# Two layers of a four-branch decoder trunk: the last recurrence unit's serial steps as block diagonal products of the whole array

## The chip, the cores and the metric

The kernel runs on one core of a Trainium2 chip. The core has five engines that run on their own and meet through semaphores: TensorE multiplies matrices (PE in the profile, and PEld for its loading of weights), VectorE (DVE), ScalarE (ACT) and GpSimd (POOL) do elementwise work, SyncE (SP) issues DMAs. The metric is the device time of one execution in microseconds (us), and the median of several executions is what counts.

TensorE holds one operand of a product, the weights, and streams the other one through. In the profile a form such as `128*128 128x512` says how large the array is that the product uses (rows * columns) and how large the streamed operand is. `64*64` is one quarter of the array.

## The reference

Two layers, each with four parallel branches that read the same 512 tokens of 1024 channels. The change lies in one branch, the RWKV-7 time mixing, whose core is a recurrence over tokens, for 8 heads of width 64:

```python
def step(state, inp):
    r_t, w_t, k_t, v_t, a_t, b_t = inp
    sa = jnp.einsum('bhvk,bhk->bhv', state, a_t)
    state = (state * w_t[:, :, None, :] + sa[..., None] * b_t[:, :, None, :]
             + v_t[..., None] * k_t[:, :, None, :])
    return state, jnp.einsum('bhvk,bhk->bhv', state, r_t)
...
_, y = lax.scan(step, s0, xs)
y_mu = jnp.mean(y, -1, keepdims=True)
y_var = jnp.mean(jnp.square(y - y_mu), -1, keepdims=True)
y = ((y - y_mu) * lax.rsqrt(y_var + RWKV_GN_EPS)).reshape(B, S, W) * lnx_g + lnx_b
```

The other branches are latent attention, a convolution module and cross-attention into a memory. Each branch's output is gated, projected to 1024 channels, weighted by a sigmoid of the layer's input and added up; one more projection, the residual and a layer norm end the layer.

## The kernel before

**Tiles and streams.** All large products run on TensorE with operands split into a high and a low part, three products for one (`mm3`): tiles `ps_m` (merge gates), `po` (branch projections), `ps_rg` (gates of the recurrence branch), `pz` (last projection). These make up one long stream of items, written out at the end of `layer_items`. Each product of that stream has the form 128*128 with a streamed operand of 128x512.

**The recurrence in units.** The scan is turned into chunks of 64 tokens. `rwkv_unit(j0, hf, rkv)` (L764) treats two pairs of heads (`SUB`, index `s`) over 256 tokens, that is 4 chunks; `un = j0 + hf` numbers the four units of a layer 0 to 3, and units 1 and 3 go on with the state that units 0 and 2 left. The two heads of a pair lie on partitions 0 to 63 and 64 to 127 (`HALF`). Within a unit the order is: small products of 64x64 that solve within each chunk (tiles `g`, `x0`, `x1`, `x2`, `va`), then `gb`, from which VectorE makes for every chunk the transition `Gs` (identity added), the input `H` and the readout `B` (L1062 to L1069); then the serial steps (L1073 to L1089): in each, `w = Gs^T state` on TensorE, then `S = w * decay + H` on VectorE. Step c+1 reads the S of step c. Unit 3 has three such steps, c = 0, 1, 2. Then the readout `yb` (L1093), the statistics over each head (`bn_stats`, `bn_aggr`, L1109 to L1115), a power on GpSimd, the normalisation on ScalarE, and transposes `ty` back (L1125). All products inside a unit are quarter-array products (`64*64`); in a step, four of them: two pairs of heads by two heads.

**What sets the order.** The program is written out by a planner in Python: `Plan` keeps a clock for each engine from a table of costs, and the order in which it emits instructions is the program order on each engine. The stream of large products is the filler; units and other side work are tasks, each of which says what it waits for when it yields. A task that yields "pe" is taken up as soon as its time has come on TensorE's clock; one that yields "small" moreover waits until `GATHER` = 1500 ns have passed since the array was last used in quarters (L161), so that quarter-array work of several tasks goes out in one group. One that yields "slack" waits until VectorE's planned clock is reached (L157): other work on VectorE goes first. `plan.due` sets a task's time to that at which given tiles are ready. `shape` (L110) charges the switch of the array between quarters and whole. `MM` (L271) chooses the cost of a product by its form; the one for a full-precision product of the whole array is 1.667 ns for each streamed column and 5 ns more (L284).

**Counters.** `L["chains"]`, `L["backs"]`, `L["ends"]`, `L["units"]` count, within a layer, the units that have gone through the readout, the solve, the transposes, and everything. Tiles in the recurrence's pool carry tags, and one tag with `bufs=1` is one buffer: `Q`, `M` and `T` are such tags, and `yb` takes `T` (L1099).

**The stream around unit 3.** In layer 0 unit 3 comes while the third branch's merge items (`ps_m`, `po`) run, in layer 1 while the recurrence branch's gate items (`ps_rg`) run. The gated outputs of the recurrence branch are needed by the last merge items, `merge_items(0, ...)`, which stand behind the four `ps_rg` items and two `ps_m` items.

Of the kernel before, what the change touches and what calls it, by code (L numbers as in the profile page):

```python
# [16 lines left out]
ALU = mybir.AluOpType  # L17
# [181 lines left out]
def _names(*aps):  # L199
    return [a.tensor.name for a in aps if hasattr(a, "tensor")]  # L200
# [65 lines left out]
def trunk_kernel(ctx: ExitStack, tc: tile.TileContext, A, out, dbg=None):  # L266
    nc = tc.nc
    plan = Plan(tc.keep_in_program_order)
    V, S, G = Engine(plan, nc.vector, "DVE"), Engine(plan, nc.scalar, "ACT"), Engine(plan, nc.gpsimd, "POOL")

    def MM(o, lhsT, rhs, start, stop, four=False):  # L271
        n = 1
        for d in rhs.shape[1:]:
            n *= d
        k, m = lhsT.shape[0], lhsT.shape[-1]
        plan.shape(64 if k <= 64 else 128, 64 if m <= 64 else 128)
        if max(k, m) <= 64:
            c = max(0.42 * n + 1.0, 29.0) if four else max(0.83 * n + 12.0, 59.0)
        elif rhs.dtype != F32 or n < 16:
            c = max(0.4167 * n + 13.0, 109.0) * (2 if rhs.dtype == F32 else 1)  # L280
        elif m <= 64:
            c = 0.83 * n + 3.0
        else:
            c = 1.667 * n + 5.0  # L284
        plan.op("PE", c, _names(o), _names(lhsT, rhs))
        plan.keep(nc.tensor.matmul(o, lhsT, rhs, start=start, stop=stop))  # L286
# [13 lines left out]
    def pool(bufs, **k):  # L300
        return Space(plan, ctx.enter_context(tc.tile_pool(bufs=bufs, **k)), bufs)
# [8 lines left out]
    pa = pool(2, name="pa", space=PSUM)  # L310
# [28 lines left out]
    def cc(n):  # L339
        return cst[:, CCOL[n][0]:CCOL[n][1]]  # L340
# [227 lines left out]
    HALF = [slice(0, 64), slice(64, 128)]  # L568
# [70 lines left out]
    def layer_items(l):  # L639
        items = []  # L640
        L = {}
# [109 lines left out]
        SUB = range(2)  # L751

        def chunks(ap):

            return ap.rearrange("p (a b) w -> p b a w", b=2)

        def by2(ap):
            return ap.rearrange("p (a b) w -> p a b w", a=2)
# [5 lines left out]
        def rwkv_unit(j0, hf, rkv):  # L764
            t = f"_{l}_{j0}_{hf}"
            un = j0 + hf
# [6 lines left out]
            def rk(tag, shape, name=None, dt=F32, bufs=1):  # L773
                return L["rp"].tile([128] + shape, dt, tag=tag, name=(name or tag) + t, bufs=bufs)
# [27 lines left out]
            bt, kt, w = rk("bt", [2, 256]), rk("kt", [2, 256]), rk("s4", [2, 256], "w")  # L802
# [16 lines left out]
            for s in SUB:  # L819
                for cp, c2, h in quads:  # L820
                    c = 2 * cp + c2
                    MM(g0[HALF[c2], h, 128 * s + 64 * cp:128 * s + 64 * cp + 64], bt[HALF[h], s, 64 * c:64 * c + 64], AR[HALF[h], s, c, 0], start=True, stop=True, four=True)
            for s in SUB:
                for cp, c2, h in quads:
                    c = 2 * cp + c2
                    MM(g0[HALF[c2], h, 256 + 2 * s + cp:257 + 2 * s + cp], sq[HALF[h], s, 64 * c:64 * c + 64], bones2[HALF[h], h:h + 1], start=True, stop=True, four=True)
            gvs = [g1[:, :, 256 * s:256 * s + 256].rearrange("p h (a w) -> p h a w", a=2) for s in SUB]
            for s in SUB:
                for cp, c2, h in quads:
                    c = 2 * cp + c2  # L830
# [7 lines left out]
            M = rk("M", [8, 65]).rearrange("p c w -> p (c w)")[:, 0:512].rearrange("p (s c w) -> p s c w", s=2, c=4)  # L838
            gm = g0[:, :, 0:256].rearrange("p h (s c w) -> p s h c w", s=2, c=2)
            for cp in range(2):  # L840
                V.tensor_tensor(out=M.rearrange("p s (a b) w -> p s a b w", b=2)[:, :, :, cp], in0=gm[:, :, ::-1, 1] if cp else gm[:, :, :, 0],
                                in1=rn[:, :, cp:4:2].unsqueeze(3).to_broadcast([128, 2, 2, 64]), op=ALU.mult)
# [55 lines left out]
            for s in SUB:  # L898
                yield "slack"
                V.tensor_tensor(out=NQ[s].rearrange("p (h a) m w -> p h a (m w)", h=2), in0=gvs[s],  # L900
                                in1=mask.unsqueeze(1).unsqueeze(1).to_broadcast([128, 2, 2, 128]), op=ALU.mult)
# [38 lines left out]
            def place(tag, name):  # L940
# [12 lines left out]
            T, Q, Zd = (rk(n, [2, 4, 64]) for n in "TQZ")  # L953
            V.tensor_tensor(out=T.rearrange("p s c (b t) -> p (s c) b t", b=4), in0=tc_.unsqueeze(2).to_broadcast([128, 8, 4, 16]),
                            in1=bm.unsqueeze(1).unsqueeze(3).to_broadcast([128, 8, 4, 16]), op=ALU.mult)
# [13 lines left out]
            for s in SUB:  # L969
                for cp, c2, h in quads:  # L970
                    c = 2 * cp + c2
# [47 lines left out]
                    MM(x2[HALF[h ^ cp], 1, s, c2, h], NQ[s][HALF[c2], 2 * h + cp, 0], vt[s][HALF[c2], 2 * h + cp], start=True, stop=True, four=True)  # L1019
            L["backs"] += 1  # L1020
            yield
            Z = rk("Z", [2, 4, 64], "Zi")
            for c2, copy in ((0, S.copy), (1, V.tensor_copy)):
                copy(Z.rearrange("p s (a b) w -> p b s a w", b=2)[:, c2], x2[:, 0, :, c2])
                for s in SUB:
# [6 lines left out]
            for s in SUB:  # L1032
                for cp, c2, h in quads:
                    MM(va[HALF[c2], s, h ^ cp, cp], Z[HALF[h ^ cp], s, 2 * cp + c2], RA[s][HALF[h ^ cp], 2 * c2 + h], start=True, stop=True, four=True)
            yield
# [7 lines left out]
            gb, hh, y0 = ([x[:, :, a:b].rearrange("p c (a w) -> p c a w", a=2) for x in gbs] for a, b in ((0, 256), (256, 384), (384, 512)))  # L1043
            for s in SUB:
                for cp, c2, h in quads:
                    MM(gb[s][HALF[h], c2, cp], VA[s][HALF[c2], 2 * (h ^ cp) + cp, 64:128], BP[s][HALF[c2], 2 * h + cp], start=True, stop=True, four=True)
                for cp in range(2):
                    for first in (True, False):
                        for c2 in range(2):
                            for h in range(2):  # L1050
                                e = 2 * h + cp
                                x, y = (bk1[s][:, e], vt[s][:, e]) if first else (BP[s][:, e, 0:64], VA[s][:, 2 * (h ^ cp) + cp, 0:64])
                                MM(hh[s][HALF[h], c2, cp], x[HALF[c2]], y[HALF[c2]], start=first, stop=not first, four=True)
                for h in range(2):
                    for first in (True, False):
                        for cp in range(2):
                            for c2 in range(2):
                                e = 2 * h + cp
                                x, y = (NQ[s][:, e, 1], vt[s][:, e]) if first else (BP[s][:, e, 64:128], VA[s][:, 2 * (h ^ cp) + cp, 0:64])
                                MM(y0[s][HALF[c2 ^ cp], c2, h], x[HALF[c2]], y[HALF[c2]], start=first, stop=not first, four=True)  # L1060
            yield
            Gs, H, B, Y0 = (rk(tag, [2, 4, 64], n) for tag, n in ((n, n) for n in ("Gs", "H", "B", "Y0")))  # L1062
            for s in SUB:
                V.tensor_tensor(out=by2(H[:, s]), in0=hh[s], in1=chunks(dl[:, 4 * s:4 * s + 4]).to_broadcast([128, 2, 2, 64]), op=ALU.mult)
                V.tensor_tensor(out=by2(Gs[:, s]), in0=gb[s][:, :, :, 0:64], in1=cc("id2")[:, 0:64].unsqueeze(1).unsqueeze(1).to_broadcast([128, 2, 2, 64]), op=ALU.add)
                S.copy(by2(Y0[:, s]), y0[s])
            for s in SUB:
                V.tensor_tensor(out=by2(B[:, s]), in0=gb[s][:, :, :, 64:128], in1=chunks(AR[:, s, :, 1, :]), op=ALU.add)
# [4 lines left out]
            states = [[zero, zero] if hf == 0 else [state[j] for s, j in js]]  # L1073
            for c in range(4):
                e = 2 * (c % 2) + c // 2
                if hf == 0 and c == 0:
                    states.append([H[:, s, 0] for s in SUB])
                elif hf == 0 or c < 3:
                    ps, = yield from pa.take([128, 2, 64], f"w{c}" + t, 1, "small")
                    for s in SUB:  # L1080
                        for half in HALF:
                            MM(ps[half, s], Gs[half, s, e], states[c][s][half], start=True, stop=True)
                    yield
                    s1 = rk("S", [2, 64], f"S{c}", bufs=4)
                    for s in SUB:
                        V.scalar_tensor_tensor(out=s1[:, s], in0=ps[:, s], scalar=dl[:, 4 * s + c], in1=H[:, s, e], op0=ALU.mult, op1=ALU.add)
                    pa.free()
                    states.append([s1[:, s] for s in SUB])
                    yield  # L1089
            for s, j in js:  # L1090
                state[j] = states[-1][s]
            yield lambda: un == 3 or L["backs"] > un + 1
            ps, = yield from pg.take([128, 2, 512], "yb" + t, 1, "small")  # L1093
            yp = ps[:, :, 0:256].rearrange("p h (s a w) -> p s h a w", s=2, a=2)
            for s in SUB:
# [11 lines left out]
            bs, mv = rk("gs", [48]), rk("gm", [16])  # L1107
            y8 = yb.rearrange("p s e w -> p (s e) w")
            for e in range(8):  # L1109
                if e % 2 == 0 and un < 3:  # L1110
                    yield "slack"
                V.bn_stats(bs[:, 6 * e:6 * e + 6], y8[:, e])
            if un < 3:
                yield "slack"
            for e in range(8):  # L1115
                V.bn_aggr(mv[:, 2 * e:2 * e + 2], bs[:, 6 * e:6 * e + 6])
# [8 lines left out]
            ps, = yield from pa.take([128, 512], "ty" + t)  # L1125
# [29 lines left out]
        def rkv_items(j):  # L1155
            def take(n, i):
                def after(ps):
                    d = u(f"{n}{j}" + t_)
                    mix(4 * i + j, ps, d)
                    rkv[j][n] = d  # L1160
                    if n == "v" and j % 2:
                        for hf in range(2):
                            plan.spawn(rwkv_unit(j - 1, hf, rkv[j - 1:j + 1]))
                return after

            for i, n in enumerate("rkv"):
                ch_item(4 * i + j, f"{n}{j}", take(n, i), lambda: "lora" in L and (j < 2 or L["read"] or room()))
# [940 lines left out]
```

## Time and profile before

| | |
|---|---|
| median of 3 runs | 1488.05 us (1487.92 to 1488.8) |
| the profiled execution, its own time | 1488.66 us |
| its span, first to last instruction | 1486.5 us |
| mean granted TensorE clock | 0.998 |
| recurrence steps of unit 3, layer 0 (starts) | 583.66, 586.31, 590.10 us |
| recurrence steps of unit 3, layer 1 (starts) | 1346.79, 1349.43, 1352.08 us |

The busy times of the profile's first part are those of all instructions of an engine, as shares of the span. Rows of a timeline give the start, the duration and the count of instructions that stand next to each other; the duration of a product runs from its start to its modelled end, and products overlap, so that the distance from one start to the next is what a product costs on a full TensorE. A bracket at the end of a row is the time that the engine sat idle before it, and what released it. A full-precision product appears as two records: the four products of a step are a row with x8.

### The profile page before, as it was taken

The numbers are of one execution on the slowest core, as the hardware profiler recorded it, in microseconds if no ns is written. First come the engines' busy times: TensorE is split into PE (matmuls) and PEld (weight loads), VectorE is DVE, ScalarE is ACT, GpSimd is POOL, SyncE is SP. The second block draws the span as 40 slices with busy tenths as digits, with TensorE's granted clock in tenths as the row PEclk, the third lists the DMA queues.
The fourth block names the chain that finished last, engine by engine and source line by source line (L and its number), as shares of the span: only waits on it lengthen the run. The fifth ranks groups of instructions, "written<-read, shape, count | busy, mean of one in ns | idle before, by whom it ended". The sixth has DMA issues, their size and how long they took to land.

```text
span 1486.5 us, 29014 instructions
## 1 busy us (share of the span) xinstructions
PE 1472.0 (99%) x11818; PEld 1232.9 (83%) x11818; DVE 1043.4 (70%) x1994; ACT 675.6 (45%) x1303; POOL 144.2 (10%) x329
## 2 busy tenths in 40 slices
PE   9999999999999999999999999999999999999997
PEld 8888888888888887888999888888888788888886
DVE  5799998755757666545554899997866476757747
ACT  5546653425354534343264465623454354444331
POOL 0000000020403030000010000000040203121002
PEclk9999999999999999999999999999999999999999
DMA  6444342332232222433353252332232313233532
GB/s 215 137 125 101 86 125 85 99 75 89 73 91 73 84 82 89 127 118 129 112 164 109 75 147 65 115 102 97 89 95 76 95 49 107 68 103 118 163 96 78
DMA packets 89158, 153.50 MB, mean 103 GB/s; under 512 B 41025, under 2 KB 47425, under 8 KB 89025
## 3 DMA queue, kind: packets, MB, share of 16 engines
q1 hardware_dynamic: 89024, 151.65, 34.3%
q8 instruction: 93, 1.52, 0.4%
q14 instruction: 41, 0.33, 0.1%
HBM read 134.32 MB, written 5.77 MB: 94 GB/s over the span
## 4 chain that ended last, share of the span: by engine, by line
PE 91%; DVE 4%; ACT 1%; DMA 1%; POOL 1%; issue 1%; SPq 0%; DVEq 0%; ACTq 0%; POOLq 0%
PE ps_m L286 24%; PE po L286 12%; PE ps_cg L286 3%; PE ps_xg L286 3%; PE ps_rg L286 3%; PE ps_xq L286 3%; PE ps_mg L286 3%; PE ps_glu L286 3%; PE ps_v L286 3%; PE ps_val L286 3%; PE ps_r L286 2%; PE pz L286 2%; PE ps_k L286 2%; PE ms L286 2%; PE pl L286 2%; PE x L286 1%
## 5 line engine op out<-in xcount | busy, mean ns | idle before, releaser
L235 DVE SCALAR_TENSOR_TENSOR cacc<-hpad,prm,cacc 128x512 f32<-128x512 f32 x240 | 178.9, 748 | 4.0
L235 ACT ACTIVATE tm<-ps_m,prm 128x512 f32<-128x512 f32 x64 | 44.1, 689 | 160.1 <-PE ps_m L286 159.9
L235 DVE SCALAR_TENSOR_TENSOR mt<-tm,po 128x512 f32<-128x512 f32 x48 | 32.9, 686 | 89.8 <-PE po L286 89.7
L235 POOL TENSOR_TENSOR tmpW<-ZT,W 64x14 f32<-64x14 f32 (+6 forms) x112 | 44.2, 395 | 8.0
L235 ACT ACTIVATE mP<-ms,nmm 128x128 f32<-128x128 f32 (+3 forms) x64 | 33.8, 529 | 22.2 <-DVE nmm L235 17.2
L235 POOL TENSOR_SCALAR ZT<-W 64x256 f32<-64x256 f32 x8 | 6.3, 783 | 359.4 <-DMA W<-scr 317.4
L235 POOL TENSOR_TENSOR ZT<-ZT,tmpW 64x14 f32<-64x14 f32 (+6 forms) x112 | 38.9, 348 | 8.8
L235 DVE TENSOR_TENSOR merged<-merged,mt 128x512 f32<-128x512 f32 x48 | 33.2, 692 | 1.7
L235 ACT COPY mPT<-mt 128x128 f32<-128x128 f32 (+3 forms) x64 | 26.8, 427 | 15.2 <-PE mt L291 14.1
L235 POOL MEMSET D<- 128x8 f32 x8 | 0.9, 117 | 332.7 <-PE ms L286 316.7
L235 DVE TENSOR_REDUCE nmm<-ms 128x1 f32<-128x128 f32 (+3 forms) x64 | 30.7, 484 | 0.1
L235 DVE SCALAR_TENSOR_TENSOR merged<-tm,po 128x512 f32<-128x512 f32 x16 | 11.0, 685 | 26.6 <-PE po L286 26.6
L235 POOL TENSOR_SCALAR lrs<-lmv 128x1 f32<-128x1 f32 x8 | 4.0, 501 | 252.6 <-DVE lmv L235 247.6
L291 PE MATMUL mt<-cst,mP 128*128 128x128 f32 x160 | 27.7, 275 | 0.3
L235 DVE TENSOR_SCALAR mP<-mP,smm 128x128 f32<-128x128 f32 (+3 forms) x64 | 24.8, 387 | 2.3
L235 POOL TENSOR_SCALAR gr<-gm 128x8 f32<-128x8 f32 x8 | 2.8, 353 | 223.9 <-DVE gm L235 223.9
L235 ACT ACTIVATE yb<-yb,mr,gr 128x64 f32<-128x64 f32 x64 | 22.1, 430 | 2.4 <-DVE mr L235 2.4
L291 PEld LDWEIGHTS mt<-cst,mP 128*128 128x128 f32 x160 | 18.9, 141 | 4.9 <-issue 1.4
L286 PE MATMUL ms<-kTl,qT 96*128 96x128 f32 (+3 forms) x64 | 22.0, 344 | 0.0
L235 ACT ACTIVATE z<-z,lnb,lrs 128x256 f32<-128x256 f32 (+2 forms) x11 | 7.0, 666 | 30.3 <-DVE lnb L235 30.3
L235 ACT ACTIVATE xP<-xs,nmx 128x256 f32<-128x256 f32 x32 | 15.2, 476 | 12.1 <-DVE nmx L235 11.6
L286 PE MATMUL ms<-kTh,qT 96*128 96x128 f32 (+3 forms) x64 | 20.6, 322 | 0.0
(3575 smaller groups left out, 5251.8 us busy)
## 6 DMA issues: line engine op xcount, KB each, us to landing
w<-in_w_ch_dram SPq DMA_DIRECT2D x146, 512.0 KB, 3.6
w<-in_w_o_dram SPq DMA_DIRECT2D x32, 512.0 KB, 3.6
w<-in_w_out_dram SPq DMA_DIRECT2D x16, 512.0 KB, 3.5
w<-in_w_lat_dram SPq DMA_DIRECT2D x15, 336.0 KB, 3.0
w<-in_w_mk_dram SPq DMA_DIRECT2D x8, 512.0 KB, 3.5
w<-in_w_mv_dram SPq DMA_DIRECT2D x8, 512.0 KB, 3.7
w<-in_w_qk_dram SPq DMA_DIRECT2D x8, 320.0 KB, 3.0
x<-in_xT_dram SPq DMA_DIRECT2D x8, 256.0 KB, 6.2
```

The source lines that it names most:

```text
L235: return self.plan.keep(f(*a, **k))
L286: plan.keep(nc.tensor.matmul(o, lhsT, rhs, start=start, stop=stop))
L291: plan.keep(nc.tensor.transpose(o, i, ident))
```

## The change

Only unit 3 of each layer is treated differently. Two tiles `Gd0` and `Gd1` of 128 partitions by 4 chunks by 128 columns, one for each pair of heads, take the place of `Gs`: the transition of the first head stands in the upper left 64x64, that of the second in the lower right, and GpSimd writes zeros in the other two quarters. They use the buffers of tags `Q` and `M`. A serial step is then one product of the whole array for each pair of heads (weights 128x128, streamed operand 128x64) instead of two of a quarter. Filling takes four additions on VectorE in place of two. The steps are emitted under "pe", after a wait in the planner for the matrix and the state, and no longer under "small". The readout of unit 3 waits in the planner until three units have passed their transposes. The statistics of unit 2 are no longer under "slack".

```diff
             L["backs"] += 1
             yield
+            diag = [rk("Q", [2, 4, 64], "Gd0").rearrange("p s c w -> p (s c w)"), rk("M", [8, 65], "Gd1").rearrange("p c w -> p (c w)")[:, 0:512]] if un == 3 else None
+            if diag:
+                diag = [x.rearrange("p (c w) -> p c w", c=4) for x in diag]
+                for x in diag:
+                    for i in range(2):
+                        G.memset(x[HALF[i], :, 64 - 64 * i:128 - 64 * i], 0.0)
             Z = rk("Z", [2, 4, 64], "Zi")
...
-            Gs, H, B, Y0 = (rk(tag, [2, 4, 64], n) for tag, n in ((n, n) for n in ("Gs", "H", "B", "Y0")))
+            Gs = None if diag else rk("Gs", [2, 4, 64])
+            H, B, Y0 = (rk(n, [2, 4, 64]) for n in ("H", "B", "Y0"))
...
-                V.tensor_tensor(out=by2(Gs[:, s]), in0=gb[s][:, :, :, 0:64], in1=cc("id2")[:, 0:64].unsqueeze(1).unsqueeze(1).to_broadcast([128, 2, 2, 64]), op=ALU.add)
+                eye = cc("id2")[:, 0:64].unsqueeze(1).unsqueeze(1).to_broadcast([128, 2, 2, 64])
+                for i in range(2) if diag else ():
+                    V.tensor_tensor(out=by2(diag[s][HALF[i], :, 64 * i:64 * i + 64]), in0=gb[s][HALF[i], :, :, 0:64], in1=eye[HALF[i]], op=ALU.add)
+                if not diag:
+                    V.tensor_tensor(out=by2(Gs[:, s]), in0=gb[s][:, :, :, 0:64], in1=eye, op=ALU.add)
...
-                    ps, = yield from pa.take([128, 2, 64], f"w{c}" + t, 1, "small")
+                    ps, = yield from pa.take([128, 2, 64], f"w{c}" + t, 1, "pe" if diag else "small")
+                    if diag:
+                        plan.due(*(x for s in SUB for x in (diag[s], states[c][s])))
+                        yield "pe"
                     for s in SUB:
-                        for half in HALF:
+                        if diag:
+                            MM(ps[:, s], diag[s][:, e], states[c][s], start=True, stop=True)
+                        for half in () if diag else HALF:
                             MM(ps[half, s], Gs[half, s, e], states[c][s][half], start=True, stop=True)
...
-            yield lambda: un == 3 or L["backs"] > un + 1
+            yield lambda: L["ends"] >= un if un == 3 else L["backs"] > un + 1
...
-                if e % 2 == 0 and un < 3:
+                if e % 2 == 0 and un < 2:
                     yield "slack"
                 V.bn_stats(bs[:, 6 * e:6 * e + 6], y8[:, e])
-            if un < 3:
+            if un < 2:
                 yield "slack"
```

## The prediction

> **What bounds the kernel now.** I read the page's totals and its chain first, then the span in stretches, then the timeline around the steps of unit 3.
>
> ```profile
> span 1486.5 us, 29014 instructions
> PE 1472.0 (99%) x11818; PEld 1232.9 (83%) x11818; DVE 1043.4 (70%) x1994; ACT 675.6 (45%) x1303; POOL 144.2 (10%) x329
> PE 91%; DVE 4%; ACT 1%; DMA 1%; POOL 1%; issue 1%; SPq 0%; DVEq 0%; ACTq 0%; POOLq 0%
> ```
> ```profile
> core 0: us, PE busy (x) PEld busy (x) DVE busy (x) ACT busy (x) POOL busy (x), PEclk, DMA share, GB/s
> 400.00:600.00 200.00, 199.09 (x2506) 163.30 (x2505) 126.55 (x296) 91.41 (x185) 38.52 (x88) 1.00 0.29 81
> 600.00:1400.00 800.00, 798.58 (x6233) 670.52 (x6232) 547.64 (x1017) 362.45 (x688) 69.68 (x155) 1.00 0.35 106
> 1400.00:1470.00 70.00, 70.00 (x311) 57.96 (x310) 45.32 (x83) 19.82 (x27) 3.25 (x6) 1.00 0.29 91
> ```
>
> TensorE is busy for 1472.0 of 1486.5 us and makes up 91% of the chain that ended last. From 600 to 1400 us it is idle for 800 - 798.58 = 1.42 us, and not at all from 1400 to 1470. So whatever waits for a recurrence step waits behind other products, and a shorter chain of steps by itself earns nothing. The change is worth what it takes from, or adds to, the time that TensorE spends on the steps, plus any new wait of TensorE.
>
> ```profile
> 583.12 0.39 PE L286 MATMUL ps_m<-xh,w90h 128*128 128x512 f32 x1
> 583.35 0.39 PE L286 MATMUL ps_m<-xh,w90l 128*128 128x512 f32 x1
> 583.66 0.45 PE L286 MATMUL w<-S,Gs 64*64 64x64 f32 x8
> 584.04 0.50 PE L286 MATMUL ps_m<-xl,w90h 128*128 128x512 f32 x1
> 584.38 0.39 PE L286 MATMUL ps_m<-xh,w90h 128*128 128x512 f32 x1
> ...
> 586.31 0.45 PE L286 MATMUL w<-S,Gs 64*64 64x64 f32 x8
> 586.69 0.50 PE L286 MATMUL po<-ycg2l,w91h 128*128 128x512 f32 x1
> ...
> 588.19 0.60 PE L291 MATMUL ty<-cst,yb 128*128 128x128 f32 x4
> ...
> 590.10 0.45 PE L286 MATMUL w<-S,Gs 64*64 64x64 f32 x8
> 590.48 0.50 PE L286 MATMUL po<-ycg2l,w91h 128*128 128x512 f32 x1
> ...
> 592.75 0.69 PE L286 MATMUL yb<-S,B 64*64 64x64 f32 x32
> ```
> ```profile
> 1346.47 0.39 PE L286 MATMUL ps_rg<-xh,w214l 128*128 128x512 f32 x1
> 1346.79 0.45 PE L286 MATMUL w<-S,Gs 64*64 64x64 f32 x8
> 1347.17 0.50 PE L286 MATMUL ps_rg<-xl,w214h 128*128 128x512 f32 x1
> 1347.51 0.39 PE L286 MATMUL ps_rg<-xh,w214h 128*128 128x512 f32 x1
> ...
> 1349.43 0.45 PE L286 MATMUL w<-S,Gs 64*64 64x64 f32 x8
> ...
> 1352.08 0.45 PE L286 MATMUL w<-S,Gs 64*64 64x64 f32 x8
> ```
>
> These are the six steps of unit 3, three in each layer. Each stands alone between two products of the large stream: no other quarter-array work shares its group. A large product follows the one before it after 0.23 us (583.12 to 583.35). With a step in between, the way from 583.35 to 584.38 takes 1.03 us for two large products; 1.03 - 2 x 0.23 = 0.57 us is what a lone step costs TensorE, 0.38 us of it from the start of the step to the next large product, the rest the turn of the array into quarters and back. Layer 1 gives the same: 1346.47 to 1347.51 is 1.04 us. **Six steps cost 6 x 0.57 = 3.4 us**, the most that the change can take from the products themselves.
>
> **The new step.** It has two products of the whole array in full precision with 64 streamed columns. No row shows that form, so it is bounded. An x8 row for four products shows two records for one product; I count four records for a new step.
>
> ```profile
> 117.17 0.28 PE L286 MATMUL ms<-kTh,qT 96*128 96x128 f32 x1
> 117.28 0.27 PE L286 MATMUL ms<-kTh,qTl 96*128 96x128 f32 x1
> ...
> 135.69 2.40 PE L286 MATMUL mo<-mPT,v 128*64 128x128 f32 x40
> 138.02 0.33 PE L291 MATMUL mt<-cst,mP 128*128 128x128 f32 x1
> ```
>
> The lower bound comes from the other full-precision product over all 128 rows, `mo`: 40 records from 135.69 to 138.02, 2.33 / 40 = 0.058 us each, so 4 x 0.058 = 0.23 us for a step. That row has weights of only 64 columns, though. With weights of 128 columns the `ms` products, 128 streamed columns in one pass, follow each other after 0.11 us, though a large product streams four times as many columns in 0.23 us, twice the time; there the loading of the weights sets the pace. By that row a new step costs 4 x 0.11 = 0.44 us. If each product of this form needed four records in place of two, it would be 0.87 us. **I take 0.44**: the new weights have 128 columns as those of `ms` have, and 64 streamed columns cannot cover a load which 128 do not. No turn of the array is left to pay, since the neighbours use the whole array too. A step falls from 0.57 to 0.44, 0.13 us; **six give -0.8 us**. The bounds give 6 x (0.23 - 0.57) = -2.0 us and 6 x (0.87 - 0.57) = +1.8 us.
>
> [...]
>
> **VectorE.** Filling the matrices takes four additions where two stood.
>
> ```profile
> 580.04 0.41 DVE L235 TENSOR_TENSOR Gs<-gb,cst 128x256 f32<-128x256 f32 x1
> 580.37 0.41 DVE L235 TENSOR_TENSOR H<-gb_1x,dl 128x256 f32<-128x256 f32 x1
> ...
> 584.16 0.48 DVE L235 SCALAR_TENSOR_TENSOR S<-w,dl,H 128x64 f32<-128x64 f32 x2 [2.06 <-PE w L286]
> ...
> 595.83 1.10 DVE L235 BATCH_NORM_STATS2 gs<-yb 128x6 f32<-128x64 f32 x8
> 596.85 0.62 DVE L235 BATCH_NORM_AGGREGATE gm<-gs 128x2 f32<-128x6 f32 x8
> ```
> ```profile
> L235 DVE SCALAR_TENSOR_TENSOR mt<-tm,po 128x512 f32<-128x512 f32 x48 | 32.9, 686 | 89.8 <-PE po L286 89.7
> ```
>
> One takes 0.33 us from its start to the next (580.04 to 580.37), and the half-height ones stream the same 256 elements, so two more are 0.66 us a layer, 1.3 in all. VectorE has 2.06 us of idle time right behind, and TensorE runs large products meanwhile: cost nothing. Without that cover it would be the 1.3 us. The statistics of unit 2 that now go first are 1.10 + 0.62 = 1.7 us of VectorE work; queued behind them are a merge's addition from `po` and the low part of a weight that is loaded ahead. Who would wait is the large output after next, since these take turns in two banks: the one in between lasts 24 x 0.23 = 5.5 us for a `ps_m` item and 12 x 0.23 = 2.8 us for a `po`, and the emptying of `po`, 0.69 us, behind 1.7 us of statistics needs 2.4: nothing. Were something else ahead of it as well, a `po` would start late, by at most the 1.7 us.
>
> **GpSimd.** Four memsets of 64x256 a layer.
>
> ```profile
> 579.89 0.20 POOL L235 TENSOR_SCALAR gr<-gm 128x8 f32<-128x8 f32 x1 [30.40 <-DVE gm L235]
> 1346.81 0.20 POOL L235 TENSOR_SCALAR gr<-gm 128x8 f32<-128x8 f32 x1 [34.79 <-DVE gm L235]
> ...
> L235 POOL TENSOR_SCALAR ZT<-W x8: 400/788/1212, 312.5 to 1298.1; 64x256 f32<-64x256 f32 x8
> ```
>
> The nearest row, a scaling of 64x256, takes 0.79 us, so 3.2 us; from below, nothing. GpSimd is idle for 30.40 and 34.79 us before its next work in the two layers, and the matrices' additions come only at 580.04: hidden. Without cover, up to 3.2 us of unit 3, still behind large products.
>
> **The waits.** Steps no longer wait for `GATHER`. The readout of unit 3 waits in the planner for the transposes of unit 2, which stood at 588.19, ahead of the readout at 592.75, and come sooner now; nothing on an engine waits, the stream goes on. No DMA is moved, and SP's queue keeps its order. The unit ends some us earlier, which by the idle time above is worth nothing.
>
> **Sum.** 1488.66 (the profiled execution's own time) - 0.8 = 1487.9; that execution lies 0.6 above the median of 1488.05, so the forecast for a median is **1487.2 us**. What a measurement can tell from no change is 0.2%, 3.0 us, thus 1485.1 to 1491.0.
>
> **The rivals.** (a) Cheap products: the step costs 0.23, -2.0 us, 1486.0. For it: the rate of `mo`, and the kernel's own cost table. Against: its weights are half as wide. (b) Dear products: four records each, +1.8, 1489.9. Against: every full-precision row here has two. (c) The other side of the line: TensorE waits. Its queue is in order, and a step placed "pe" has less large work between itself and the S that it needs.
>
> ```profile
> PE tk L291 <- DVE S L235: 1.2, 1, 1.2
> PE w L286 <- DVE S L235: 0.8, 1, 0.8
> ```
>
> The second row shows this wait once, 0.8 us. It decides as soon as fewer than four large products (4 x 0.23 = 0.9) stand between a step and the next, because S takes 0.12 us to start behind the step and 0.48 for the pair (584.04, 584.16). Six gaps of 0.8 (two between steps and one before the readout, in each layer) less 0.8 are +4.0: 1492.1. Behind each waiting step stand all large products of the stream. Against: the step is placed only when the planner reckons S done and adds its latency. (d) A luckier order downstream: from 400 to 1400 us TensorE is idle 0.91 + 1.42 = 2.3 us; if the new order closed all of it as well, -3.1 in all, 1485.0, just beyond the line. Against: the stream is the same list, and only these tasks move. That the change does not do what it says (the steps still alone with turns of the array) would leave 1488.0 and falls into the forecast.
>
> **How the numbers follow.** Forecast 0.46, (a) 0.20, (b) 0.12, (c) 0.12, (d) 0.10. Faster is (d), 0.10; slower is (c), 0.12; the rest, 0.78, lies within 0.2%. The range runs from (d) at 1485.0 to just above (b) at 1490.2, and leaves out (c) and what of (d) falls below.
>
> **What would show it.** Right: the six steps as 128*128 rows of x4, a large product following a step's start after 0.44 us and no gaps of 0.31 or 0.34 around; VectorE with 0.66 us more before the first S; TensorE's idle time in 600 to 1400 near 1.4 us. The page's busy time of TensorE falls by less than 2 us. Wrong: rows of idle time before `w` on PE with S as releaser, records of x8 for the new steps, a step at 0.23, or a late `po`.

## The result and the profile after

The changed kernel takes 1491.19 us in the median of 18 executions (1489.34 to 1492.5), the kernel before 1488.24 us in 18 executions beside them (1487.83 to 1489.2). The ratio is 1.0017, with a 95% interval of 1.0011 to 1.0023: some 2.9 us slower, about the 0.2% that this kernel's measurement can tell, and every execution is longer than the longest of before. The profiled execution took 1492.5 us, 3.8 more than that of before.

The page of the changed kernel, its totals, its instruction queues and its chain (the last by engine):

```profile
span 1490.6 us, 28980 instructions
PE 1473.1 (99%) x11794; PEld 1235.6 (83%) x11794; DVE 1045.7 (70%) x1998; ACT 676.2 (45%) x1303; POOL 146.5 (10%) x337
...
q8 instruction: 93, 1.52, 0.4%
q14 instruction: 40, 0.33, 0.1%
...
PE 85%; DVE 5%; DMA 3%; ACT 3%; POOL 2%; issue 1%; SPq 0%; DVEq 0%; ACTq 0%; POOLq 0%
```

TensorE has 24 products fewer and yet is busy for 1.1 us longer, and its share of the chain fell from 91% to 85%. DMA, VectorE, ScalarE and GpSimd have the difference: something off TensorE ended last for a while. The span in the same stretches as before (columns as there) says where:

```profile
600.00:1400.00 800.00, 795.69 (x6201) 669.13 (x6201) 542.42 (x1003) 360.97 (x685) 69.78 (x160) 1.00 0.36 105
1400.00:1470.00 70.00, 70.00 (x311) 57.97 (x310) 47.82 (x90) 21.50 (x29) 1.57 (x3) 1.00 0.27 86
```

Between 600 and 1400 us TensorE is idle for 800 - 795.69 = 4.31 us, where it was 1.42. The timeline of TensorE around the steps of unit 3, first in layer 0 and then in layer 1:

```profile
585.50 0.40 PE L286 MATMUL po<-ycg1h,w91l 128*128 128x512 f32 x1
585.73 0.56 PE L286 MATMUL w<-S,Gd 128*128 128x64 f32 x4
586.09 0.47 PE L286 MATMUL po<-ycg2l,w91h 128*128 128x512 f32 x1
586.41 0.39 PE L286 MATMUL po<-ycg2h,w91h 128*128 128x512 f32 x1
...
1354.52 0.56 PE L286 MATMUL w<-S,Gd 128*128 128x64 f32 x4
...
1356.36 0.55 PE L286 MATMUL w<-S,Gd 128*128 128x64 f32 x4
```

The way over two large products and a step, 585.50 to 586.41, is 0.91 us; less 2 x 0.23 a step costs 0.45 us, where an old one cost 0.57. (The next large product follows the step's start after 0.36 us and takes 0.32 itself in place of 0.23; the forecast had the cost right and put it all into the first of these.) No step of unit 3 has idle time ahead of it. So the steps did what they were made for, and the loss is elsewhere. The waits of TensorE name it (total, times, longest):

```profile
PE w L286 <- DVE S L235: 2.3, 1, 2.3
PE warm L286 <- POOL reset L235: 1.3, 1, 1.3
PE tk L291 <- DVE S L235: 1.2, 1, 1.2
```

One wait of 2.3 us for a state S is new; the other two are as long in the kernel before. It isn't in unit 3. It stands at 1258 us, in unit 1 of layer 1, whose steps are quarter products as before. The timeline of TensorE there, of before:

```profile
1258.16 0.39 PE L286 MATMUL ps_m<-xh,w202l 128*128 128x512 f32 x1
1258.49 0.52 PE L286 MATMUL w<-S,Gs 64*64 64x64 f32 x8
1258.80 0.69 PE L286 MATMUL x<-Z,P 64*64 64x64 f32 x32
1259.32 0.64 PE L286 MATMUL x<-P,PT 64*64 64x64 f32 x32
```

and of the changed kernel:

```profile
1258.12 0.39 PE L286 MATMUL ps_m<-xh,w202l 128*128 128x512 f32 x1
1260.78 0.57 PE L286 MATMUL w<-S,Gs 64*64 64x64 f32 x6 [2.27 <-DVE S L235]
...
1261.23 1.07 PE L286 MATMUL x<-Z,P 64*64 64x64 f32 x30
1261.99 1.17 PE L286 MATMUL x<-P,PT 64*64 64x64 f32 x32
```

The last large product starts within 0.04 us of its old time; up to there the change had cost nothing. Then TensorE stands still for 2.27 us, and the products behind the gap take longer: from the start of `x<-Z,P` (its first records, left out above, start at 1261.09) to that of the next group 0.90 us where it was 0.52, and the group after that has 1.17 in place of 0.64. The stretches of 2 us of the changed kernel give the granted clock (the third column from the right):

```profile
1258.00:1260.00 2.00, 0.51 (x3) 0.08 (x1) 1.56 (x2) 0.64 (x3) 0.00 (x0) 1.00 0.00 0
1260.00:1262.00 2.00, 1.22 (x41) 1.23 (x45) 1.86 (x7) 0.41 (x3) 0.00 (x0) 0.71 0.76 246
1262.00:1264.00 2.00, 2.00 (x47) 1.88 (x42) 0.77 (x2) 0.31 (x2) 0.00 (x0) 0.50 0.04 16
1264.00:1266.00 2.00, 2.00 (x27) 1.47 (x28) 0.52 (x1) 1.56 (x4) 0.00 (x0) 0.94 0.00 0
```

Behind the gap the granted clock falls to 0.50. In windows of 0.25 us it is 1.00 up to 1260.75, 0.50 from 1261.00 to 1264.25 and 1.00 again from there. The three stretches from 1260 us on make (0.29 + 0.50 + 0.06) x 2 / 0.50 = 3.4 us at half clock, which cost at most half of that, 1.7 us. What they did cost is read from the start of the next step, of before and of the changed kernel:

```profile
1261.87 0.33 PE L286 MATMUL w<-S,Gs 64*64 64x64 f32 x4
```
```profile
1265.60 0.38 PE L286 MATMUL w<-S,Gs 64*64 64x64 f32 x5
```

From step to step it is 3.38 us before (1258.49 to 1261.87) and 4.82 after (1260.78 to 1265.60): 1.4 us for the slower clock. With the wait ahead of it, the way from the last large product to the second of these steps grows from 3.71 to 7.48 us, by 3.8 us, as much as lies between the two profiled executions.

**Why S is late.** S of that step is VectorE's, and VectorE was held up by what stood ahead of it, back to a DMA. The issues on SP's queue (start, time on the queue) and the first ScalarE row that reads the weight w198, of before:

```profile
1213.25 2.69 SPq L298 DMA_DIRECT2D w<-in_w_ch_dram  x2
1222.07 0.38 SPq L298 DMA_DIRECT2D scr<-Mc  x1
1224.24 0.47 SPq L298 DMA_DIRECT2D W<-scr  x1
```
```profile
1216.76 1.05 ACT L235 CAST w198h<-w 128x1024 fp32r<-128x1024 f32 x1 [1.05 <-DMA w<-in_w_ch_dram]
```

and of the changed kernel:

```profile
1213.21 2.69 SPq L298 DMA_DIRECT2D w<-in_w_ch_dram  x2
1223.51 0.38 SPq L298 DMA_DIRECT2D scr<-Mc  x1
1227.39 0.47 SPq L298 DMA_DIRECT2D W<-scr  x1
```
```profile
1218.29 1.05 ACT L235 CAST w198h<-w 128x1024 fp32r<-128x1024 f32 x1 [2.65 <-DMA w<-in_w_ch_dram]
```

The weight is asked for at the same time. It can be cast 3.51 us later before and 5.08 us later after: 1.6 us lost. The matrix `Mc` of the solve goes through DRAM behind it (`scr<-Mc`, then `W<-scr`), and the reading back, which waits for the writing to land (2.15 us after its issue before, 3.87 after), is issued 2.17 us behind the writing before and 3.88 after: 1.7 us more. GpSimd's triangular solve begins 3.2 us late, its result goes through DRAM once more, the high and low parts of w203 and w204 slip behind it on ScalarE and VectorE, and the S of the second step of unit 1, which came just in time before, is 2.3 us late. The row of that S, of before and of the changed kernel:

```profile
1258.16 0.47 DVE L235 SCALAR_TENSOR_TENSOR S<-w,dl,H 128x64 f32<-128x64 f32 x2
```
```profile
1260.45 0.47 DVE L235 SCALAR_TENSOR_TENSOR S<-w,dl,H 128x64 f32<-128x64 f32 x2
```

**What is in the way of these two transfers.** On every engine the instructions between layer 0's unit 3 and layer 1's unit 3 stand in the same order in both kernels, so neither SP nor any engine issues anything else there. What differs is where TensorE's own instructions are fetched. The page's two instruction queues moved 1.52 + 0.33 = 1.85 MB for 28980 instructions, 64 bytes each; 2 x 11794 products and weight loads are 1.51 MB, so q8 carries TensorE's. Its 93 packets are 16.3 KB each, 256 instructions, and took 0.004 x 16 x 1490.6 / 93 = 1.0 us each. An old step has 8 products with 8 weight loads, a new one 4 with 4: behind layer 0's three steps TensorE has used up 24 instructions less, and each later packet is asked for 24 instructions later. In windows of 1 us of the DMA view, the packet near w198's issue lies between 1212 and 1213 us before, ahead of the issue at 1213.25, and between 1214 and 1215 after, behind the issue at 1213.21. The second one lies between 1220 and 1221 before, ahead of `scr<-Mc`, and between 1224 and 1225 after, inside the way from `scr<-Mc` to `W<-scr`. What the changed kernel moved from 1214 to 1215 us, by queue (packets, MB, share of 16 engines):

```profile
q1 hardware_dynamic: 31, 0.13, 74.4%
q8 instruction: 1, 0.02, 11.1%
```

That is so far two things at the same place. The experiments test whether one makes the other.

### The profile page after: what moved, and what is told of

The parts are those of the page before. It is cut to its first block, busy times and chain, and to the rows that moved or that the text cites. A ratio compares the mean times of both kernels' runs of the same rounds, so it can differ in the third digit from the quotient of the medians.

```text
span 1490.6 us, 28980 instructions
## 1 busy us (share of the span) xinstructions
PE 1473.1 (99%) x11794; PEld 1235.6 (83%) x11794; DVE 1045.7 (70%) x1998; ACT 676.2 (45%) x1303; POOL 146.5 (10%) x337
## 3 DMA queue, kind: packets, MB, share of 16 engines
q8 instruction: 93, 1.52, 0.4%
## 4 chain that ended last, share of the span: by engine, by line
PE 85%; DVE 5%; DMA 3%; ACT 3%; POOL 2%; issue 1%; SPq 0%; DVEq 0%; ACTq 0%; POOLq 0%
PE ps_m L286 22%; PE po L286 11%; PE ps_xq L286 3%; PE ps_mg L286 3%; PE ps_rg L286 3%; PE ps_v L286 3%; PE ps_xg L286 3%; PE ps_val L286 3%; PE ps_glu L286 3%; PE ps_r L286 2%; PE ps_k L286 2%; PE pz L286 2%; PE pl L286 2%; PE ms L286 2%; PE ps_cg L286 2%; DMA w<-in_w_ch_dram 1%
```

## The experiments

A number in brackets behind a ratio is its 95% interval.

**The changed kernel once more**, unaltered.

> The changed kernel once more. Theory T (a transfer lands late at the second step of unit 1 in layer 1, where no slack is left, and it does so in most executions of this program): TensorE waits 1.5 to 2.5 us for S between 1255 and 1265 us again, and the ratio stays near 1.002. Rival C (the profiled execution was an unlucky one, and the slower median has another cause): no such wait in this profile, the ratio still near 1.002, and the loss stands at another place of the trace.

1490.43 us (1489.21 to 1492.41), ratio 1.0014 [1.0005, 1.0023]. The wait is there again, at the same product, with 1.6 us; this time the clock stays at 1.00 behind it.

```profile
1258.76 0.52 PE L286 MATMUL w<-S,Gs 64*64 64x64 f32 x8 [1.55 <-DVE S L235]
```

The cast of w198h came 5.31 us after the issue and `W<-scr` 3.64 us after `scr<-Mc`. So it isn't an accident of one trace, and the slower clock comes on top in some executions only.

**The change in layer 1 alone.**

```diff
-... if un == 3 else None
+... if un == 3 and l == 1 else None
...
-            yield lambda: L["ends"] >= un if un == 3 else L["backs"] > un + 1
+            yield lambda: (L["ends"] >= un or l != 1) if un == 3 else L["backs"] > un + 1
...
-                if e % 2 == 0 and un < 2:
+                if e % 2 == 0 and un < (2 if l == 1 else 3):
```

> The change in layer 1 alone; up to 1338 us the program is that of before. If the loss comes from what the change in layer 0 does to the time of all that follows (theory T), this one is not slower: 1487.7 to 1488.3, the three steps of layer 1 giving -0.4. If the new order in layer 1 is what costs (rival L: among it the order in which weights and norm constants are fetched after 1360 us), it is slower by 1.5 to 3 us.

1487.62 us (1486.68 to 1488.91), ratio 0.9996 [0.9987, 1.0005]. The longest wait for S at a step is 0.4 us, cast and issue are 3.46 us apart. The change in layer 1, with all that it moves there on SP's and VectorE's queues, costs nothing.

**The change in layer 0 alone**: the same edit with `l == 0`.

> The change in layer 0 alone; the order of every engine after unit 3 of layer 0 is that of before, only some 0.4 us earlier. Theory T: slower by 2 to 3 us, with the wait of TensorE for S between 1255 and 1265 us. Rival L: 1487.6 to 1488.2, no wait.

1492.15 us (1489.98 to 1494.2), ratio 1.0024 [1.0015, 1.0034], the whole loss.

```profile
1258.60 0.52 PE L286 MATMUL w<-S,Gs 64*64 64x64 f32 x8 [1.64 <-DVE S L235]
```

The edit ends at 600 us, every instruction behind it stands as in the kernel before, and 650 us later the same step waits. Beside that, TensorE stops for 0.84 us at 1344 us with nothing to wait for that the profile shows, which the profile calls `issue`:

```profile
1344.82 0.34 PE L286 MATMUL gb_1x<-VA,BP 64*64 64x64 f32 x5 [0.84 <-issue]
```

**The kernel before once more**, unaltered.

> The kernel before once more, for a second profile: how far the landing of the weights and of the blocks of the substitution at 1213 to 1250 us differs between two executions of one program. If theory T holds for the program and not for the execution, the cast of the weight that started at 1216.8 us starts within 0.3 us of that again and TensorE does not wait at 1258 us; if a single execution decides, it may be 1.5 us later here too.

1488.84 us in one execution. Cast and issue of w198 are 3.57 us apart, `scr<-Mc` and `W<-scr` 2.17: the landing repeats within 0.1 us, where the changed kernel lost 1.5.

The next four change nothing but the count of TensorE instructions ahead of everything: the 18 warm-up products at the start of the kernel, which take the time until the first input has come, are replaced by more narrow or fewer wide ones. A warm-up product is two instructions.

**The changed kernel with its 24 instructions given back.**

```diff
     for i in range(18):
-        MM(warm[:, 0:256], reset[:, 0:128], reset, start=True, stop=True)
+        plan.op("PE", 0.4167 * 256 + 13.0, _names(warm), _names(reset))
+    for i in range(30):
+        plan.keep(nc.tensor.matmul(warm[:, 0:152], reset[:, 0:128], reset[:, 0:152], start=True, stop=True))
```

> The changed kernel with the 18 warm-up products of 256 columns at its start replaced by 30 of 152 columns: 12 bf16 products more, which is 24 TensorE instructions more, at about the same 3.8 us of time. Every instruction behind them stands as in the changed kernel; only the count of instructions ahead of each is back to that of the kernel before from layer 0's unit 3 on. Theory F (the shorter stream shifts TensorE's 16 KB instruction fetches into the transfer of weight w198): the fetch near 1212 us comes before the issue of w198 again, the CAST of w198h starts about 3.6 us after the issue instead of 5.1, TensorE's wait for S in unit 1 of layer 1 falls from 2.3 to at most 0.5 us, and the time is 1487.0 to 1488.4 (before less the 0.7 us of six cheaper steps). Rival P (the chip's landing times or the phase of the end of layer 0's unit 3 itself, not the count of instructions): wait of 1.6 to 2.3 us stays, 1490.5 to 1491.5. Rival M (memsets and diagonal fills make a scratch transfer late): as rival P.

1487.58 us (1487.02 to 1488.69), ratio 0.9998 [0.9989, 1.0006]. The loss is gone, with each instruction of the change in its place:

```profile
1217.41 1.05 ACT L235 CAST w198h<-w 128x1024 fp32r<-128x1024 f32 x1 [1.14 <-DMA w<-in_w_ch_dram]
```
```profile
1213.82 2.69 SPq L298 DMA_DIRECT2D w<-in_w_ch_dram  x2
...
1222.64 0.38 SPq L298 DMA_DIRECT2D scr<-Mc  x1
1224.81 0.47 SPq L298 DMA_DIRECT2D W<-scr  x1
```

3.59 us from issue to cast, 2.17 us over the scratch, and no wait of TensorE for S at any step in the list. Memsets, diagonal fills and new steps are all still there, which rules them out.

**The kernel before with 18 instructions taken away**, without any of the change.

```diff
     for i in range(18):
-        MM(warm[:, 0:256], reset[:, 0:128], reset, start=True, stop=True)
+        plan.op("PE", 0.4167 * 256 + 13.0, _names(warm), _names(reset))
+    for i in range(9):
+        plan.keep(nc.tensor.matmul(warm, reset[:, 0:128], reset.unsqueeze(1).to_broadcast([128, 2, 256]), start=True, stop=True))
```

> The kernel before, untouched but for its warm-up: 9 products of 512 columns in place of 18 of 256, so 18 TensorE instructions fewer ahead of everything, none of the change in it. Theory F: the fetch that stood 1 us ahead of the issue of w198 now stands inside its transfer, the CAST of w198h starts about 5 us after the issue, TensorE waits 1 to 2.5 us for S at the first steps of unit 1 in layer 1, and the time is 1489.7 to 1491.7, slower than before without any of the change. Rivals P and M: as the kernel before, 1487.8 to 1488.8.

1490.21 us (1488.52 to 1492.19), ratio 1.0012 [1.0003, 1.0021]: slower, within the range that was given. The way there was only half as expected. The first packet stands in w198's transfer, and the cast comes late:

```profile
1217.93 1.04 ACT L235 CAST w198h<-w 128x1024 fp32r<-128x1024 f32 x1 [2.43 <-DMA w<-in_w_ch_dram]
```
```profile
1213.05 2.69 SPq L298 DMA_DIRECT2D w<-in_w_ch_dram  x2
```

4.88 us. The second packet still comes ahead of `scr<-Mc`, and that way keeps its 2.17 us. With one of the two delays instead of both, the waits for S come to 0.6 us in all, in two places; the larger part of the loss in this trace is an `issue` stop of 1.0 us at 1344 us, as in the kernel with layer 0's edit alone:

```profile
1345.05 0.21 PE L286 MATMUL gb_1x<-vt,NQ 64*64 64x64 f32 x1 [1.01 <-issue]
```

In these two traces the dense group of quarter products (tiles `gb`, `gb_1x`) begins at 1341.0 and 1341.2 us, and an instruction packet starts 1.0 and 1.1 us behind its beginning; in the kernel before the group begins at 1340.9 and the packet starts with it, and there is no stop. The changed kernel and its repetition, which stop for 0.3 and 0.6 us in this group, have their packet 0.9 and 1.0 us behind its beginning; in the other traces of this order, none of which stops here, it starts within 0.3 us of it. So the stop is most likely one for instructions; no row names what ends it.

**The changed kernel with half of them given back**: as the first of these four, with 24 products of 190 columns.

> As the first, with 24 warm-up products of 190 columns: 12 TensorE instructions more than the changed kernel, half of what it took away. Theory F: the fetch lies between the two places, about 0.5 us after its old place relative to the issue of w198, so at its edge: 1487.5 to 1490.5, and the wait for S goes with the start of w198h's CAST (3.6 us after the issue: no wait; 5.1: a wait of 1.6 to 2.3). Rivals P and M: 1490.5 to 1491.5 whatever the fetch does.

1488.28 us (1487.48 to 1489.31), ratio 1.0002 [0.9993, 1.0011]. The cast is 3.50 us after the issue, `W<-scr` 2.18 after `scr<-Mc`, and there is no wait for S and no stop at 1344 us (one `issue` stop of 0.35 us stands at 1196 us, in another group of quarter products). Twelve instructions decide over the wait.

**The kernel before with 24 instructions added**, the control for the narrow warm-up, **and once more for a second trace.**

> The kernel before with the warm-up of 30 products of 152 columns, a control for the first: 24 instructions more ahead of everything. If a warm-up of many narrow products saves time by itself, this is faster than before by the same amount as the first kernel is faster than the changed one. Theory F: fetches come about 1.5 us earlier than in the kernel before, further ahead of w198, so 1487.6 to 1488.8 with no wait over 0.5 us for S there, unless an earlier fetch meets another transfer that has as little margin. Rivals P and M: the same time as before.

> The kernel before with the warm-up of 30 narrow products once more, for a second trace: its median was 1489.7 where 1487.6 to 1488.8 was expected, and its first trace was of its fastest run and showed no loss. Theory F: another transfer is met in some runs; if this run is over 1489.5, the trace names a wait of 1 us or more behind a transfer that landed late, with a fetch inside it, most likely w203 (a fetch stood at 1246 us, its cast was at about 1247). If the narrow warm-up itself costs: TensorE's lateness is there already at 100 us, over 1 us more than in the first trace.

1489.71 us (1488.77 to 1492.15), ratio 1.0014 [1.0005, 1.0022], and 1490.59 in the single later execution. A warm-up of narrow products saves nothing by itself, so the recovery of the changed kernel isn't its doing. But this kernel came out slower than expected. Neither trace shows a late w198 (3.37 and 3.50 us from issue to cast), a wait for S at a step, or an `issue` stop, and the guess that w203 is met fell. The traces do show another late weight, w14, in the first layer. In the seven traces without more instructions ahead it is cast 3.5 to 3.7 us after its issue, in the five with 12 or 24 more, the recovered kernels among them, after 4.8 to 5.5 us. The row of before (issue at 55.14) and of the second of these traces (issue at 54.87):

```profile
58.71 1.05 ACT L235 CAST w14h<-w 128x1024 fp32r<-128x1024 f32 x1 [0.77 <-DVE w13l L235]
```
```profile
60.19 1.05 ACT L235 CAST w14h<-w 128x1024 fp32r<-128x1024 f32 x1 [2.52 <-DMA w<-in_w_ch_dram]
```

In three of the five an instruction packet starts 1.1 to 2.1 us behind the issue: there the padding has moved the meeting to another transfer. TensorE falls behind by 0.2 to 1.0 us at 62 to 64 us in all five. But the recovered kernel loses most there, 1.0 us, and isn't slower in the end, so this alone doesn't explain the 1.5 us. The second trace loses another 1.4 us between 150 and 200 us, which no other trace does, and the cause is open.

Where the first packet lies against the issue of w198, and the second against `scr<-Mc`, in eight traces of this order (times in us; windows of 1 us):

| kernel | first packet in | issue of w198 | issue to cast | second packet in | `scr<-Mc` | `scr<-Mc` to `W<-scr` | median less that of before |
|---|---|---|---|---|---|---|---|
| before | 1212 to 1213 | 1213.25 | 3.51 | 1220 to 1221 | 1222.07 | 2.17 | |
| layer 1 alone | 1213 to 1214 | 1214.06 | 3.46 | 1221 to 1222 | 1222.88 | 2.18 | -0.5 |
| after, 24 given back | 1213 to 1214 | 1213.82 | 3.59 | 1221 to 1222 | 1222.64 | 2.17 | -0.6 |
| after, 12 given back | 1212 to 1213 | 1213.15 | 3.50 | 1221 to 1222 | 1221.97 | 2.18 | +0.1 |
| before less 18 | 1214 to 1215 | 1213.05 | **4.88** | 1222 to 1223 | 1223.15 | 2.17 | +2.0 |
| after | 1214 to 1215 | 1213.21 | **5.08** | 1224 to 1225 | 1223.51 | **3.88** | +2.9 |
| after, again | 1213 to 1214 | 1211.88 | **5.31** | 1223 to 1224 | 1222.41 | **3.64** | +2.3 |
| layer 0 alone | 1213 to 1214 | 1211.64 | **4.95** | 1222 to 1223 | 1221.80 | **3.69** | +4.0 |

Eight traces, sixteen places: where the packet comes behind the issue, the transfer lands 1.4 to 1.8 us later; where it comes ahead of it, it doesn't. (In windows of 0.5 us the first packet of the two rows with 1213 to 1214 and no delay lies before 1213.5, ahead of the issue.) In the four other traces of this order, the kernel before once more and the other three with 24 instructions more, both packets come ahead; the cast comes 3.4 to 3.7 us after the issue and `W<-scr` 2.2 us after `scr<-Mc`.

Other weights of 512 KB show how far this goes. In the twelve traces with the planner as it was, 886 of them (of the tensor `in_w_ch_dram`) are issued while no other transfer is under way. With no instruction packet starting in the 2.8 us behind the issue (769 of them) the weight lands after 3.5 us in the median, and 19 of 20 land within 4.3 us. With one starting 1.0 to 2.2 us behind the issue (14, the four late w198 among them) all land late, after 4.1 to 5.5 us. With one starting in the first 1.0 us (71) they land after 3.5 to 5.2 us, 4.1 in the median; with one starting later (32), after 3.5 us in the median. So a packet costs from nothing to some 2 us, by when in the transfer it comes.

**More time for landings in the planner**, in the changed kernel and in the one before: it takes a transfer to land 3.0 us after its last byte in place of 1.5.

```diff
-        self.end("DMA", self.wires + 1500.0, outs, ins)
+        self.end("DMA", self.wires + 3000.0, outs, ins)
```

> The changed kernel with one number of its planner altered: it takes a transfer to land 3.0 us after its last byte is sent in place of 1.5, so that whatever waits for a transfer is placed later in TensorE's order and other products are placed ahead of it (some 1300 of 7000 rows of TensorE's order move). Theory F (the loss is a landing 1.5 us later than planned, twice, and no margin for it): with that margin built in, the wait for S at unit 1 of layer 1 is under 0.5 us although the fetches still stand in the transfers, and the time is 1486.5 to 1488.8, unless the new order costs up to 1.5 us elsewhere. If the margin is no remedy (each late landing simply meets the next wait): 1490 to 1492.

> The kernel before with the same altered number, to stand beside the first of this group: their orders differ almost only in the changed steps. Theory F: 1487.2 to 1489.5, and 0.4 to 1.0 us slower than the first, the worth of six cheaper steps where late landings cost nothing. If the changed step is worth nothing or less by itself, this is not slower than the first.

1512.87 us (1510.75 to 1514.06), ratio 1.0163 [1.0149, 1.0177], and 1515.26 us (1513.14 to 1520.32), ratio 1.0184 [1.0167, 1.02]. As a remedy it fails far outside every expectation. The first one's stretches show TensorE idle for 13.9 us between 600 and 1400, and its list of waits is headed by one of 5.5 us ahead of the transposes of a unit's output:

```profile
600.00:1400.00 800.00, 786.07 (x6493) 658.61 (x6483) 540.58 (x1046) 358.36 (x692) 76.22 (x167) 0.99 0.35 102
```
```profile
PE ty L291 <- ACT yb L235: 6.0, 4, 5.5
```

The number moves everything that waits for any transfer, not the one chain that lacks a margin, and the new order has new places without one; which of them cost what wasn't followed further. A margin for the one chain alone (its weight asked for earlier) wasn't tried.

**The recovered changed kernel on another occasion.**

> The changed kernel with 30 warm-up products of 152 columns once more, on another occasion, to see whether its median of 1487.6 (0.6 under the kernel before, inside the interval of one comparison) comes back. Theory F: the fetches stand ahead of w198 and of the scratch write again, the CAST of w198h starts 3.4 to 3.7 us after the issue, no wait over 0.5 us for S at unit 1 of layer 1, and the time is 1487.2 to 1488.0, 0.4 to 1.0 under the kernel before. If the first result was luck of that chip: 1488.5 or more.

1488.42 us (1487.76 to 1489.56) against 1488.64 beside it, ratio 1.0 [0.9991, 1.0009]; w198 is cast 3.72 us after its issue and no step waits. The loss stays away. The gain of 0.6 us over the kernel before shrank to 0.2 and lies inside the interval both times: no version here is shown to beat the kernel before.

## Why the prediction was wrong

The forecast was 1487.2 us, no change that can be measured; the kernel is 2.9 us slower, outside the range.

- **What bounds the kernel**: right. TensorE had 1.42 us of idle time in 800, and what the change was worth had to come out of its products or of a new wait. It was a new wait.
- **The new step at 0.44 us**: right, 0.45, by four records of 0.11 with weights of 128 columns, in both layers alike. The rivals with 0.23 and 0.87 fell. The loads of the new step start 0.11 us apart (585.73, 585.84, 585.95), as those of `ms` do before (117.11, 117.22); that the loading sets the pace is the reading of such rows. Of the time put down to the turn of the array, the part ahead of the step is gone (0.31 us from the large product to the step before, 0.23 after), the part behind it stayed (0.34 before, 0.32 after), though the new step uses the whole array. Over layer 0's steps the changed kernel gains 0.37 us, as three times 0.12 would have it: it is 0.11 us behind the kernel before at the large product at 583.12 us and 0.26 ahead when w93 is first used, at 598 us.
- **VectorE's fills, GpSimd's memsets, unit 2's statistics at nothing**: right that they are hidden, since no wait of TensorE at unit 3 answers to them, and the changed kernel with its instructions given back does all of it and loses nothing. The fills were sized too small. A half-height fill starts the next 0.44 us on:

```profile
579.20 0.42 DVE L235 TENSOR_TENSOR H<-gb,dl 128x256 f32<-128x256 f32 x1
579.53 0.85 DVE L235 TENSOR_TENSOR Gd<-gb,cst 64x256 f32<-64x256 f32 x2
580.41 0.42 DVE L235 TENSOR_TENSOR H<-gb_1x,dl 128x256 f32<-128x256 f32 x1
```

  From the first fill to the next H is 0.88 us where it was 0.33, so 1.1 us more in a layer, not 0.66. The four memsets of a layer take 1.4 us (569.51 to 570.87), under the bound of 3.2.
- **"No DMA is moved, and SP's queue keeps its order"**: not so behind unit 3 of layer 1, where some weights and the norm's transfers change places; layer 1 alone shows that it costs nothing. Between the two units 3 it holds.
- **The waits, "nothing"**: the step that failed. It asked what stands in another place in the program and priced that. The wait came at a step that the change doesn't touch, in a stretch where no instruction was moved, because the length of TensorE's stream is itself a term: 24 instructions fewer in layer 0 put two 16 KB fetches into two transfers of layer 1, each of which landed 1.6 to 1.7 us later, onto a chain that ended with no margin. So the term put at nothing was, in the profiled execution, a wait of 2.3 us and 1.4 us of slower clock behind it. Rival (c) had the waiting pair right, `w` behind S, and nearly its price (4.0 against the 3.8 read above), but its place was between unit 3's steps, with the shorter spacing as the reason. Neither is what happened, so the near price is chance.
- **The change by itself**, -0.8 us in the sum, comes to 6 x 0.12 = -0.7 us by the rows of the steps. The medians don't show it: -0.5 (layer 1 alone), -0.6, +0.1 and -0.2 in the runs whose fetches miss w198 and the scratch transfer, with intervals that all include no change, and -2.4 between the two kernels with later landings, whose ranges overlap.

Shown by the runs: with the change in place, the count of instructions ahead decides over the two late landings and the wait; without it, 18 fewer bring the first late landing and waits of 0.6 us in all. Not shown by any row: what the packet does inside the transfer, and why one that starts 1.0 to 2.2 us behind the issue costs most.

## What to carry to other kernels

Where one engine is busy 99% of the time, an edit that adds or drops instructions can also move the later instruction packets of that engine (here 24 fewer moved one from the window of 1212 to 1213 us, ahead of the issue of w198, to that of 1214 to 1215, behind it); before a loss of a few microseconds is put down to the edit, pad the stream back to its old count at a place where it costs nothing, and see whether the loss stays. Pad the kernel before as well: here 24 instructions more made it 1.5 us slower by themselves, for a reason that stays open. A chain with transfers in it that ends just in time (here S at 1258.16 for a product at 1258.49) is a place where anything shows, however far away the edit is, so the places without margin belong in a prediction's range. And a difference that comes from such a place says nothing of the edit's worth in the next version of the kernel.

## What the runs showed of the hardware

- In the changed kernel q8, TensorE's instruction queue by the count of bytes, moved 93 packets of 16.3 KB, one for 256 instructions at 64 bytes each. In the twelve traces a 512 KB weight issued while no other transfer is under way lands 3.5 us after its issue in the median when no such packet starts in the 2.8 us behind the issue, and 4.1 to 5.5 us after it in all 14 cases where one starts 1.0 to 2.2 us behind it.
- In one dense group of quarter products TensorE stood still for 0.3 to 1.0 us (stops at 1344 to 1348 us) in the four traces whose packet starts 0.9 to 1.1 us behind the group's beginning, and not in the eight where it starts within 0.3 us of it. No row names what ended the stop.
- A gap of 2.27 us was followed by a granted clock of one half for 3.4 us, which cost 1.4 us; a gap of 1.55 us at the same product left the clock at 1.00.
- A full-precision product with weights of 128 columns and 64 streamed columns comes to 0.22 us, two records of 0.11.
